# An encoder of two layers in one launch: x's two halves in one padded tile, other places for the weights' tiles, and a reordered beginning and end

## The chip, the cores and the metric

The kernel runs on one core of a Trainium2 chip. The metric is the time of one execution on the device in microseconds, as the median of several runs. The engines of the core are named as in the profile: PE (TensorE, matrix products; PEld is its loading of weights), DVE (VectorE), ACT (ScalarE), POOL (GpSimd) and SP (SyncE, which here only issues transfers). Memory on the chip is SBUF, with 128 partitions; products land in PSUM.

## What is computed

A sequence of 512 positions, 1024 features wide, goes through two layers. Each layer is a mixer and an MLP, both added to x; layer 0 mixes by stick-breaking attention, layer 1 by a gated linear recurrence. At the end there is a norm.

```python
def rms_norm(x, g):
    y = x * rsqrt(mean(x * x, axis=-1, keepdims=True) + EPS)
    return y * g

for layer in range(2):
    h = rms_norm(x, norm_mix[layer])
    if layer == 0:
        y = stick_breaking_attention(h, sb_w_qkv[0], sb_w_o[0])
    else:
        y = rglru_block(h, rg_w_in[0], conv_w, conv_b, w_a, b_a, w_x, b_x, lam, rg_w_o[0])
    x = x + y
    h = rms_norm(x, norm_mlp[layer])
    x = x + square(relu(h @ w1[layer])) @ w2[layer]        # 1024 -> 4096 -> 1024
return rms_norm(x, norm_final)
```

All is float32.

## The kernel before

**Every product in three.** A float32 operand is split into a high and a low half, each in the format fp32r: `wh` is a cast of the raw weights on ACT, `wl` the difference raw - wh on DVE. The same is done to the activations: x times its norm's gains lies in `xgh` and `xgl` (`halves`, L126), mixer outputs and MLP hidden values in `bh` and `bl` (and `sh`, `sl`). `three` (L217) then issues three matmuls: wh with the high half, wl with the high half, wh with the low half. In a matmul one operand is loaded into PE as 128 columns of weights (the stationary or loaded operand) and the other one is streamed through, 256 or 512 columns long. In `three` the weights slab is loaded and x is streamed.

**Stages.** (1) A beginning, in which x and the first slabs of weights arrive and the first products for queries and keys start. The norm's factor is found beside them: `inverse` (L432) sums squares on PE (L436), takes the root on ACT, and on DVE makes a diagonal matrix `diag` and the factors `rp` and `rn`, which PE broadcasts (L453). (2) Attention in 8 pairs of heads, where PE's work (`fill`) is cut into steps, and the steps of scores and values are put among them at due times. `SUMS` and `BROAD` say after which fill step the two parts of `inverse` are placed. (3) The MLP of layer 0. (4) The recurrent block, in an order written out by hand. (5) The MLP of layer 1, and (6) the final norm, row block by row block, as the last products come out.

**The MLP.** The class `Mlp` does Strassen's seven products in place of eight. For the first quarter of the hidden width, `squared` (L828) computes plainly 8 slabs of `w_m1`, each with 24 matmuls of 512 columns in `dense` (L223). Then follow, in turn, a down stage (`times`, L1051, 14 steps of 12 matmuls of 512 columns) and an up stage (`up`, L956, 2 halves `p` of 7 products, each of 24 matmuls of 256 columns): down, up, down, up, down, up, down. In an up stage P1, P2 and P4 stream parts of `xgh` and `xgl`, P7 streams `xgh` and `low`, P5 and P3 stream `s41` and `low`, P6 streams parts of `bh` and `bl` and `low`; the weights are loaded. In a down stage the roles are changed: hidden values are loaded (`bh` and `bl` for the first half, `sh` and `sl` for the second, from `places`, L845) and weights are streamed. `leave` (L1185) runs after each step and issues what ACT and DVE do with its bank: in an up stage P1's bank is copied out (L1209) before P6 adds to the same bank, P4's bank goes through relu and square (L1219), and then `prepare` makes operands for a step four ahead. Inside these stages ACT and DVE run strictly in the order in which the code issues work (`Ordered`, L747), and all of it is recorded at L756.

**Places in SBUF.** Pools lay their tiles one behind the other in the order in which they are opened, so a longer tile moves everything behind it. Each of `xgh`, `xgl`, `bh` and `bl` is 16384 bytes per partition. The pool `last` (L1583) lies ahead of the tiles of layer 1's MLP only.

**The end.** `square` adds up squares of a half row block on ACT, `finish` (L1631) takes the root, scales the one half on ACT (the gains multiplied in by POOL in `scaled`, L1627), the other on DVE, and issues both stores on SP. `end` (L1649) puts these among the last products; row block 3, half 0, comes last, in two parts of 256 columns.

Of the kernel before, what the change touches and what calls it, by code (L numbers as in the profile page):

```python
# [17 lines left out]
P = 128  # L18
S = 512
# [7 lines left out]
SCALE = HD ** -0.5  # L27

# [13 lines left out]
SUMS = 5  # L42
BROAD = 9
# [18 lines left out]
def hybrid_encoder(  # L62
# [57 lines left out]
    xgh = const.tile([P, C, S], F32R, tag="xgh", name="xgh")  # L120
    xgl = const.tile([P, C, S], F32R, tag="xgl", name="xgl")
# [56 lines left out]
    def slab_parts(src, cuts):  # L178

        raw = wpool.tile([P, C, P], F32, tag="raw", name="raw", bufs=3)  # L180
        wh = wpool.tile([P, C, P], F32R, tag="wh", name="wh")
        wl = wpool.tile([P, C, P], F32R, tag="wl", name="wl")

        def fetch(i, queue=nc.sync):
            k = slice(*cuts[i : i + 2])
            queue.dma_start(out=raw[:, k, :], in_=src[:, k, :])

        def part(i, high=A.copy):
            k = slice(*cuts[i : i + 2])
# [4 lines left out]
            V.tensor_tensor(wl[:, k, :], raw[:, k, :], f(wh[:, k, :]), ALU.subtract)  # L194

        return wh, wl, fetch, part
# [93 lines left out]
    with ExitStack() as actx:  # L290
# [141 lines left out]
        def inverse():  # L432
# [9 lines left out]
            with tc.high_priority():  # L442
                norm["root"] = A.activation(rc, pc[:, :NB], AF.Sqrt, bias=eps_t, scale=1.0 / D)
                V.reciprocal(rc, rc)
                for t in range(NB):
                    ts = slice(t * P, (t + 1) * P)
                    V.tensor_scalar(diag[:, ts], ident, rc[:, t : t + 1], None, ALU.mult)
                V.tensor_scalar(rp, rc, SCALE, None, ALU.mult)
                V.tensor_scalar(rn, rc, -SCALE, None, ALU.mult)
# [289 lines left out]

    residual(w_so, "mlp0", so, so_next)  # L740
# [25 lines left out]
    class Mlp:  # L766
# [28 lines left out]
        def __init__(self, ctx, layer):  # L795
# [12 lines left out]
            self.s41 = self.bp.tile([P, C // 2, S], F32R, tag="s41", name="s41", bufs=1)  # L808
# [288 lines left out]
        def run(self, first, between, end):  # L1097
# [87 lines left out]
            def leave(i):  # L1185
# [32 lines left out]
                if name == "P4":  # L1218
                    self.A.activation(u[3], three, AF.Relu)  # L1219
                    self.square(u[3])  # L1220
                    if p:
                        last_sums(u, self.SUMS[:2])
                if later:
                    later.pop()()
# [19 lines left out]
                elif name == "P4":  # L1244
                    self.sums(p, slice(0, 2))
# [66 lines left out]
    with ExitStack() as mctx:  # L1312
# [18 lines left out]
        def end(ws, xs):  # L1331
            for i in range(2):
# [244 lines left out]

    residual(w_ro, "mlp1", begun, {4: ws["o4"]})
# [3 lines left out]
    with ExitStack() as mctx:  # L1582
        lp = mctx.enter_context(tc.tile_pool(name="last", bufs=1))  # L1583
# [26 lines left out]
        A.activation(lp.tile([P, 1], F32, tag="rt", name="early"), eps_t, AF.Sqrt)  # L1610

        ss = lp.tile([P, NB, 3], F32, tag="ss", name="ss")
        bias = lp.tile([P, NB], F32, tag="bias", name="bias")

        def square(t, h, i, cols=slice(0, S), end=False):

            junk = work.tile([P, S], F32, tag="sq", name="junk")
            A.activation(
                junk[:, cols], mlp.y(t, h)[:, cols], AF.Square, accum_out=ss[:, t, i : i + 1]
            )  # L1620
            if not end:
                A.activation(
# [4 lines left out]
        def scaled(t, h, cols=slice(0, S)):  # L1627
            y = mlp.y(t, h)[:, cols]
            G.tensor_tensor(y, y, gb[h][:, cols], ALU.mult)

        def finish(t, h, i, cut=None, last=None):  # L1631

            ts = slice(t * P, (t + 1) * P)
            rt = work.tile([P, 1], F32, tag="rt", name="rt")
            A.activation(rt, ss[:, t, i : i + 1], AF.Sqrt, bias=bias[:, t : t + 1], scale=1.0 / D)
            V.reciprocal(rt, rt)
            done, y = mlp.y(t, 1 - h), mlp.y(t, h)
            A.activation(done, done, AF.Copy, scale=rt)
            nc.sync.dma_start(out=out[ts, (1 - h) * S : (2 - h) * S], in_=done)
            with tc.issue_after(last.ins) if last else nullcontext():  # L1640
                V.scalar_tensor_tensor(
# [3 lines left out]
            if cut:  # L1645
                V.tensor_scalar(y[:, :cut], y[:, :cut], rt, None, ALU.mult)
            nc.sync.dma_start(out=out[ts, h * S : (h + 1) * S], in_=y)

        def end(ws, xs):  # L1649
            for t in range(2):  # L1650
# [13 lines left out]
            for i in range(2):  # L1664
                cols = slice(i * HS, (i + 1) * HS)
                ps = mlp.bank()[:, :HS]
                for g in range(2):
                    mlp.times("P4", g, 1, ws[g], ps, True, cols)
                mlp.collect("P4", 1, ps, cols)
                square(3, 0, 1 + i, cols, end=i == 1)  # L1670
                if i == 0:
                    scaled(3, 0, cols)
            finish(3, 0, 2, HS)
# [72 lines left out]
```

## Time and profile before

| | |
|---|---|
| median of 3 runs | 1047.62 us (1046.17 to 1047.67) |
| the profiled execution | 1047.03 us, its span 1045.3 us |
| granted clock of TensorE | 0.998 of full speed |
| one up stage, layer 0 and layer 1 | 39.42 and 39.84 us |
| last operation on the chain | ACT's scaling at 1040.54 us, 0.72 us |
| HBM | 137.41 MB read, 4.19 MB written, 135 GB/s over the span |

Times in the views are counted from the span's start. A row of a group has line, engine, operation, the tiles `out<-in`, and its number; for a matmul the first tile behind the arrow is the streamed one, the second the loaded one. A row of the waits view says who waited for whom, how long in total, how often, and the longest.

### The profile page before, as it was taken

The page shows a single profiled execution, that of the slowest core. Times are in us where ns is not written, and L with a number is a line of the kernel's source. Part 1 is how long each engine was busy: PE and PEld are TensorE (multiplying, and loading weights), DVE is VectorE, ACT ScalarE, POOL GpSimd, SP SyncE. Part 2 cuts the span into 40 slices and gives each one's busy share as a digit, 9 for nine tenths or more (in the row PEclk, how much of TensorE's full clock was granted, in tenths as well). Part 3 has the DMA queues.
Part 4 walks back from the last instruction along what each step waited for, and adds up shares of the span by engine and source line. Part 5 has one row for each costly group of instructions (what it writes and reads, how often), then busy time and mean ns, then how long its engine had stood idle before and what let it go on. Part 6 is the DMA issues. An engine that isn't in the chain of part 4 may idle for free.

```text
span 1045.3 us, 15858 instructions
## 1 busy us (share of the span) xinstructions
PE 1033.3 (99%) x5868; PEld 901.0 (86%) x5868; DVE 862.5 (83%) x1150; ACT 702.4 (67%) x1082; POOL 170.3 (16%) x235
## 2 busy tenths in 40 slices
PE   9999999999999999999999999999999999999997
PEld 7888888888888988988988888888888988988985
DVE  7788787847788898898899799984789797897897
ACT  6767676835766773773775699964755773773775
POOL 0354344420000010010011111100000010010013
PEclk9999999999999999999999999999999999999999
DMA  7755454537646667667682474353346667567563
GB/s 232 196 139 142 102 152 104 152 108 284 144 78 189 180 139 209 156 142 208 163 208 78 129 204 114 89 221 101 81 89 174 178 135 208 161 135 204 149 123 101
DMA packets 52828, 159.41 MB, mean 152 GB/s; under 512 B 6672, under 2 KB 7952, under 8 KB 52752
## 3 DMA queue, kind: packets, MB, share of 16 engines
q1 hardware_dynamic: 41808, 120.13, 35.5%
q0 software_dynamic: 10368, 37.75, 21.8%
q8 instruction: 46, 0.75, 0.3%
q10 hardware_dynamic: 576, 0.52, 0.2%
q14 instruction: 30, 0.25, 0.1%
HBM read 137.41 MB, written 4.19 MB: 135 GB/s over the span
## 4 chain that ended last, share of the span: by engine, by line
PE 85%; DVE 6%; issue 3%; DMA 3%; ACT 2%; SPq 1%; ACTq 0%; DVEq 0%; POOL 0%; POOLq 0%
PE ps_t L1060 14%; PE ps_acc L965 8%; PE ps_z L965 8%; PE ps_acc L1060 7%; PE ps_o L965 5%; PE ps_acc L221 5%; PE ps_acc L219 5%; PE ps_acc L220 5%; PE ps_z L1060 4%; PE ps_t L220 2%; PE ps_t L221 2%; PE ps_t L219 2%; PE ps_o L219 2%; PE ps_o L220 2%; PE ps_o L221 2%
## 5 line engine op out<-in xcount | busy, mean ns | idle before, releaser
L756 ACT CAST wh<-b 128x1024 fp32r<-128x1024 f32 x168 | 174.1, 1048 | 125.4 <-DVE b L756 77.7
L756 DVE TENSOR_TENSOR wl<-b,wh 128x1024 fp32r<-128x1024 f32 x168 | 203.6, 1220 | 50.4 <-ACT wh L756 50.2
L1042 POOL DMA_DIRECT2D b<-in_w_dn x40 | 35.0, 875 | 360.4 <-DVE b L756 204.5
L219 PE MATMUL ps_acc<-xgh,wh 128*128 128x512 f32 x192 | 78.5, 409 | 0.0
L214 DVE TENSOR_TENSOR wl<-raw,wh 128x512 fp32r<-128x512 f32 (+2 forms) x70 | 62.0, 912 | 18.3 <-ACT wh L212 18.2
L221 PE MATMUL ps_acc<-xgl,wh 128*128 128x512 f32 x192 | 75.2, 391 | 0.0
L220 PE MATMUL ps_acc<-xgh,wl 128*128 128x512 f32 x192 | 75.1, 391 | 0.0
L580 DVE TENSOR_TENSOR_SCAN scan<-keep,later 128x128 f32<-128x128 f32 (+1 forms) x64 | 58.6, 919 | 18.2 <-ACT keep L570 11.4
L756 ACT ACTIVATE u<-u 128x512 f32<-128x512 f32 x100 | 63.1, 632 | 6.9 <-DVE u L756 5.1
L212 ACT CAST wh<-raw 128x512 fp32r<-128x512 f32 (+2 forms) x70 | 50.6, 758 | 24.5 <-PE ps_acc L221 7.3
L584 POOL TENSOR_TENSOR w<-w,scan 128x128 f32<-128x128 f32 (+1 forms) x64 | 51.8, 812 | 58.6 <-DVE scan L580 52.0
L1042 POOL DMA_DIRECT2D b<-in_w_up x24 | 20.8, 868 | 240.6 <-DVE b L756 72.2
L756 DVE TENSOR_TENSOR b<-b,b 128x1024 f32<-128x1024 f32 x48 | 58.7, 1223 | 1.3
L756 DVE TENSOR_TENSOR u<-u 128x512 f32<-128x512 f32 (+1 forms) x92 | 54.8, 596 | 2.7 <-ACT u L756 1.1
L965 PE MATMUL ps_z<-xgh,wh 128*128 128x256 f32 x192 | 54.2, 282 | 0.0
L965 PE MATMUL ps_z<-xgh,wl 128*128 128x256 f32 x192 | 54.1, 282 | 0.0
L756 ACT CAST wh<-raw 128x1024 fp32r<-128x1024 f32 x46 | 47.9, 1046 | 9.2 <-PE ps_acc L1060 8.4
L965 PE MATMUL ps_acc<-low,wh 128*128 128x256 f32 x192 | 53.6, 279 | 0.0
L1060 PE MATMUL ps_t<-wl,sh 128*128 128x512 f32 x126 | 50.1, 398 | 0.0
L1060 PE MATMUL ps_t<-wh,sh 128*128 128x512 f32 x126 | 49.6, 394 | 0.0
L1060 PE MATMUL ps_t<-wh,sl 128*128 128x512 f32 x126 | 49.4, 392 | 0.0
L1060 PE MATMUL ps_t<-wh,bh 128*128 128x512 f32 x126 | 49.2, 391 | 0.0
(397 smaller groups left out, 3420.3 us busy)
## 6 DMA issues: line engine op xcount, KB each, us to landing
b<-in_w_dn SPq DMA_DIRECT2D x48, 512.0 KB, 4.5
b<-in_w_dn POOLq DMA_DIRECT2D x40, 512.0 KB, 5.6
b<-in_w_up SPq DMA_DIRECT2D x36, 512.0 KB, 4.7
b<-in_w_up POOLq DMA_DIRECT2D x24, 512.0 KB, 5.5
raw<-in_w_m SPq DMA_DIRECT2D x16, 512.0 KB, 4.1
raw<-in_w_dn SPq DMA_DIRECT2D x16, 512.0 KB, 4.6
raw<-in_w_in SPq DMA_DIRECT2D x16, 512.0 KB, 4.2
raw<-in_w_qk SPq DMA_DIRECT2D x12, 512.0 KB, 3.8
```

The costliest lines, as they stand in the source:

```text
L212: A.copy(wh[:, k, :], raw[:, k, :])
L214: V.tensor_tensor(wl[:, k, :], raw[:, k, :], f(wh[:, k, :]), ALU.subtract)
L219: PE.matmul(ps, wh, ah, start=start, stop=False)
L220: PE.matmul(ps, wl, ah, start=False, stop=False)
L221: PE.matmul(ps, wh, al, start=False, stop=stop)
L580: V.tensor_tensor_scan(sc[:, S - n : S][:, ::-1], keep[:, :n][:, ::-1], later[:, S - n :][:, ::-1], 1.0, ALU.mult, ALU.max,)
L584: G.tensor_tensor(wt, wt, sc[:, S - n + 1 : S + 1], ALU.mult)
L756: ins = getattr(self.e, name)(*args, **kwargs)
L965: PE.matmul(ps[:, i * HS : (i + 1) * HS], m, y, start=new and i == k == n == 0, stop=i == 1 and k == C // 2 - 1 and n == 2, skip_group_che ...
L1042: G.dma_start(out=unit[b].rearrange("p j n -> p (j n)"), in_=unit["src"](to), accum_op=ALU.add)
L1060: PE.matmul(ps, m, y[:, jj, cols], start=first and n == 0, stop=last and n == 2, skip_group_check=not new,)
```

## The change

It has four parts.

1. **Places.** `xgh` and `xgl` become two views into one tile `xg` that is `ASIDE` = 16 elements (64 bytes) longer. `x_at(ASIDE)` sets the views 64 bytes from the tile's start for attention and the recurrent block, `x_at(0)` sets them at its start for the two MLPs. `s41` gets 64 bytes of padding behind it. The pool `last` is gone; its small tiles now lie in unused columns of `colt` and in `c`.
2. **Beginning.** `SUMS` and `BROAD` go up by one step, and the low halves of the value weights are no longer issued with the high ones, but after `rn` and after the broadcast's copy.
3. **Later relu.** In an up stage's first half, relu, square and the sums for P4 are put off to the next step.
4. **End.** Its operations on ACT and DVE are issued in a fixed order, the last gain of tile row 3's other half moves ahead, the product with the final gains for tile row 3 goes from POOL to DVE, and the last store is issued by ACT.

```diff
+ASIDE = 16
...
-SUMS = 5
-BROAD = 9
+SUMS = 6
+BROAD = 10
...
-    xgh = const.tile([P, C, S], F32R, tag="xgh", name="xgh")
-    xgl = const.tile([P, C, S], F32R, tag="xgl", name="xgl")
+    x_t = const.tile([P, 2 * C * S + ASIDE], F32R, tag="xg", name="xg")
+    xgh = xgl = None
+
+    def x_at(aside):
+
+        nonlocal xgh, xgl
+        xgh, xgl = (
+            x_t[:, aside + i * C * S : aside + (i + 1) * C * S].rearrange("p (c s) -> p c s", s=S)
+            for i in range(2)
+        )
+
+    x_at(ASIDE)
...
-        def part(i, high=A.copy):
+        def part(i, high=A.copy, low=True):
...
-            if high == V.tensor_copy:
+            if high == V.tensor_copy or not low:
                 return
...
-                V.tensor_scalar(rn, rc, -SCALE, None, ALU.mult)
+                norm["signs"] = V.tensor_scalar(rn, rc, -SCALE, None, ALU.mult)
...
-                for u, name in zip(parts[4:], ("root", "copy")):
+                for u, name, then in zip(parts[4:], ("root", "copy"), ("signs", "copy")):
 
                     with tc.issue_after(norm[name].ins):
                         for i in range(2):
-                            u[3](i)
+                            u[3](i, low=False)
+                    with tc.issue_after(norm[then].ins):
+                        for i in range(2):
+                            u[3](i, None)
...
+    x_at(0)
     residual(w_so, "mlp0", so, so_next)
...
-            self.s41 = self.bp.tile([P, C // 2, S], F32R, tag="s41", name="s41", bufs=1)
+            t = self.bp.tile([P, C // 2 * S + ASIDE], F32R, tag="s41", name="s41", bufs=1)
+            self.s41 = t[:, : C // 2 * S].rearrange("p (k s) -> p k s", s=S)
...
                 if name == "P4":
-                    self.A.activation(u[3], three, AF.Relu)
-                    self.square(u[3])
+                    def fourth(u=u, three=three, p=p):
+                        self.A.activation(u[3], three, AF.Relu)
+                        self.square(u[3])
+                        if p:
+                            last_sums(u, self.SUMS[:2])
+                        else:
+                            self.sums(p, slice(0, 2))
+
                     if p:
-                        last_sums(u, self.SUMS[:2])
-                if later:
+                        fourth()
+                    else:
+                        later.append(fourth)
+                elif later:
                     later.pop()()
...
-                elif name == "P4":
-                    self.sums(p, slice(0, 2))
...
         def end(ws, xs):
+            x_at(ASIDE)
...
+    x_at(0)
     residual(w_ro, "mlp1", begun, {4: ws["o4"]})
...
-        lp = mctx.enter_context(tc.tile_pool(name="last", bufs=1))
         mlp = Mlp(mctx, 1)
...
-        def scaled(t, h, cols=slice(0, S)):
+        def scaled(t, h, cols=slice(0, S), e=G):
             y = mlp.y(t, h)[:, cols]
-            G.tensor_tensor(y, y, gb[h][:, cols], ALU.mult)
+            e.tensor_tensor(y, y, gb[h][:, cols], ALU.mult)
...
         def end(ws, xs):
             for t in range(2):
                 square(t, 0, 0)
                 scaled(t, 0)
                 square(t, 1, 1, end=True)
-                finish(t, 1, 1, last=mlp.gained)
+                rt = root(t, 1)
+                scaled_half(t, 0, rt, nc.sync)
+                whole_half(t, 1, rt, last=mlp.gained)
             for t in range(2, 4):
                 square(t, 1, 0)
-                scaled(t, 1)
+            scaled(2, 1)
             for g in range(2):
                 mlp.times("P4", g, 0, ws[g], xs[0], False)
+            mlp.collect("P4", 1, xs[1])
+            for e in (EV, EA):
+                e.turn(True)
+            mlp.V = EV
             mlp.collect("P4", 0, xs[0])
             square(2, 0, 1, end=True)
-            finish(2, 0, 1)
-            mlp.collect("P4", 1, xs[1])
...
+            mlp.collect("P4", 1, ps[0], halves[0])
+            rt = root(2, 1)
+            square(3, 0, 1, halves[0])
+            scaled_half(2, 1, rt, nc.sync)
+            whole_half(2, 0, rt)
+            mlp.collect("P4", 1, ps[1], halves[1])
+            square(3, 0, 2, halves[1], end=True)
+            scaled(3, 1, e=EV)
+            scaled(3, 0, halves[0], e=EV)
+            rt = root(3, 2)
+            whole_half(3, 0, rt, HS)
+            scaled_half(3, 1, rt, A)
```

The new helpers `root`, `scaled_half` and `whole_half` are the three parts of `finish`; `scaled_half` takes the queue on which its store is issued.

What it moves is seen in the order of the instructions. On DVE in the beginning, from the reciprocal of the norm's root on (`diag`, `rp`, `rn` go to PE's broadcast and to the scores; `wl` are low halves of value weights), before and then after:

```order
L444 RECIPROCAL rc<-rc 128x4
L194 TENSOR_TENSOR wl<-raw,wh 128x512 x2
L447 TENSOR_SCALAR diag<-ident,rc 128x128 x4
L448 TENSOR_SCALAR rp<-rc 128x4
L449 TENSOR_SCALAR rn<-rc 128x4
```

```order
L455 RECIPROCAL rc<-rc 128x4
L458 TENSOR_SCALAR diag<-ident,rc 128x128 x4
L459 TENSOR_SCALAR rp<-rc 128x4
L460 TENSOR_SCALAR rn<-rc 128x4
L205 TENSOR_TENSOR wl<-raw,wh 128x512 x2
```

The two low halves have moved from ahead of `diag` to behind `rn`. On ACT in an up stage, at the change from the first half to the second (`ps_acc` is P4's bank of the first half, `ps_z` P1's of the second), before and then after:

```order
L756 CAST bh<-u 128x2x768
L756 ACTIVATE u<-ps_acc 128x2x256
L756 ACTIVATE u<-u 128x2x256
L756 CAST wh<-b_8014 128x1024
L756 COPY u<-ps_z 128x512
L756 COPY u<-ps_o 128x512
```

```order
L771 CAST bh<-u 128x2x768
L771 CAST wh<-b_8007 128x1024
L771 COPY u<-ps_z 128x512
L771 ACTIVATE u<-ps_acc 128x2x256
L771 ACTIVATE u<-u 128x2x256
L771 COPY u<-ps_o 128x512
```

Relu and square now stand behind one cast of weights and the copy of `ps_z`; the order on DVE there is unchanged. On DVE at the end, before and then after (the four tiles `c` are the output's quarters; 7346 and, after, 7342 hold the half that comes last):

```order
L1641 SCALAR_TENSOR_TENSOR c_7346<-c_7346,rt,gb 128x512
L756 SCALAR_TENSOR_TENSOR c_7346<-ps_o,rr,c_7346 128x256
L1636 RECIPROCAL rt<-rt 128x1
L1641 SCALAR_TENSOR_TENSOR c_7346<-c_7346,rt,gb 128x256
L1646 TENSOR_SCALAR c_7346<-c_7346,rt 128x256
```

```order
L771 SCALAR_TENSOR_TENSOR c_7342<-c_7342,rt,gb 128x512
L771 SCALAR_TENSOR_TENSOR c_7342<-ps_o,rr,c_7342 128x256
L771 TENSOR_TENSOR c_7343<-c_7343,gb 128x512
L771 TENSOR_TENSOR c_7342<-c_7342,gb 128x256
L771 RECIPROCAL rt<-rt 128x1
L771 SCALAR_TENSOR_TENSOR c_7342<-c_7342,rt,gb 128x256
L771 TENSOR_SCALAR c_7342<-c_7342,rt 128x256
```

Two products that POOL did before stand on DVE ahead of the last reciprocal. The matmuls are the same 5844 in both kernels, and apart from the two parts of `inverse` they stand in the same order.

More of the change, by code (lines that the diff above doesn't have):

```diff
@@ L1625, in square, with root, leaves, scaled_half @@
                 )
-        def scaled(t, h, cols=slice(0, S)):
+        def scaled(t, h, cols=slice(0, S), e=G):
             y = mlp.y(t, h)[:, cols]
-            G.tensor_tensor(y, y, gb[h][:, cols], ALU.mult)
-        def finish(t, h, i, cut=None, last=None):
-            ts = slice(t * P, (t + 1) * P)
+            e.tensor_tensor(y, y, gb[h][:, cols], ALU.mult)
+        def root(t, i):
             rt = work.tile([P, 1], F32, tag="rt", name="rt")
[L1635 to L1639, printed above, removed]
+            EA.activation(rt, ss[:, t, i : i + 1], AF.Sqrt, bias=bias[:, t : t + 1], scale=1.0 / D)
+            EV.reciprocal(rt, rt)
+            return rt
+        def leaves(t, h, queue):
+            queue.dma_start(out=out[t * P : (t + 1) * P, h * S : (h + 1) * S], in_=mlp.y(t, h))
+        def scaled_half(t, h, rt, queue):
+            y = mlp.y(t, h)
+            EA.activation(y, y, AF.Copy, scale=rt)
+            leaves(t, h, queue)
+        def whole_half(t, h, rt, cut=None, last=None):
+            y = mlp.y(t, h)
             with tc.issue_after(last.ins) if last else nullcontext():
-                V.scalar_tensor_tensor(
+                EV.scalar_tensor_tensor(
                     y[:, cut:], y[:, cut:], rt, gb[h][:, cut:],
@@ L1645, in finish @@
             if cut:
[L1646 to L1647 removed]
+                EV.tensor_scalar(y[:, :cut], y[:, :cut], rt, None, ALU.mult)
+            leaves(t, h, nc.sync)
         def end(ws, xs):
```

25 lines of the change are left out of this document (11 added, 14 removed).

## The prediction

> **What bounds the kernel now.** I read the engine shares first, then TensorE's waits, then the chain of waits, and only then the tail.
>
> ```profile
> span 1045.3 us, 15858 instructions
> PE 1033.3 (99%) x5868; PEld 901.0 (86%) x5868; DVE 862.5 (83%) x1150; ACT 702.4 (67%) x1082; POOL 170.3 (16%) x235
> PE ps_z L965 <- ACT u L756: 1.0, 1, 1.0
> PE ps_z L453 <- DVE rn L449: 0.6, 1, 0.6
> PE ps_t L602 <- DVE tl L618: 0.4, 1, 0.4
> PE ps_z L436 <- DVE ssq L421: 0.3, 1, 0.3
> ```
>
> TensorE is busy for 99% of the span, and its waits that this change touches, the four rows above, come to 2.3 us. A change that keeps all matmuls can therefore gain only in three ways: by ending one of these waits, by shortening the tail behind the last matmul, or by making the matmuls follow each other faster. The last sounds impossible, since the granted clock is 1.00 in the windows shown further down, but the chain of waits says otherwise. It merges a run of matmuls into one row (start, length, what, count). Here is the second half of one up stage, first in layer 0 and then in layer 1; each row is one product of 24 matmuls 256 columns wide:
>
> ```profile
> 430.27 2.88 PE ps_z L965 x24
> 433.15 2.74 PE ps_o L965 x24
> 435.89 2.83 PE ps_z L965 x24
> 438.71 2.72 PE ps_o L965 x24
> ...
> 900.56 2.88 PE ps_z L965 x24
> 903.44 2.83 PE ps_o L965 x24
> 906.27 2.84 PE ps_z L965 x24
> 909.10 2.82 PE ps_o L965 x24
> 911.93 2.84 PE ps_z L965 x24
> 914.76 2.86 PE ps_o L965 x24
> 917.63 2.88 PE ps_z L965 x24
> ```
>
> The products come in the order P1, P5, P6, P3, P7, P2, P4. P1, P2 and P4 stream x's halves and take 2.86 to 2.88 us. P5 and P3 stream s41: 2.72 to 2.74 us in layer 0, but 2.82 to 2.83 in layer 1. Same code, same sizes, no wait; what differs between the layers is where s41 lies. Add up the tile sizes in pool order and take each address modulo 512 bytes: x's halves lie at 32, the weight slabs wh and wl at 288, s41 at 480 in layer 0 and at 96 in layer 1 (the pool `last` sits ahead of it there). So the distance from the loaded operand to the streamed one is 256 for x, 192 for s41 in layer 0, 320 in layer 1. The matmuls of 512 columns in the down stages depend on it as well (layer 0, then layer 1; each 12 matmuls):
>
> ```profile
> 452.75 2.72 PE ps_acc L1060 x12
> 455.47 2.75 PE ps_t L1060 x12
> ...
> 923.25 2.72 PE ps_acc L1060 x12
> 925.97 2.80 PE ps_t L1060 x12
> ```
>
> In each pair the first row loads bh (distance 256 in both layers), the second loads sh: distance 320 in layer 0, 192 in layer 1. So for 512 columns 256 is the cheap distance and 192 the dear one (2.80/12 = 233 ns a matmul against 227); for 256 columns it is the other way round, 2.73/24 = 114 ns at 192 against 2.87/24 = 120 at 256.
>
> **The change part by part: places.** The tile `xg` is 64 bytes longer than the two it replaces, so everything behind it moves by 64: wh and wl to 352, bh to 96. Outside the MLPs x begins at 96 (distance 256, as before). In the MLPs it begins at 32, so the distance becomes 192. s41 comes to 32 in both layers, since `last` is gone: 192. Its own pad puts sh and sl at 96: 256 in both layers.
>
> - Up stages, x: P1, P2 and P4 go from 2.88, 2.86 and 2.88 to s41's 2.73, P7, half of which streams x, from 2.84 to 2.73. That is 0.15 + 0.13 + 0.15 + 0.11 = 0.54 us a half, in 2 halves of 6 stages: -6.4 us. P6 streams bh and stays. No row has x at 192, so the bounds are s41's two layers: at 2.73 it is this, at 2.82 only 0.06 + 0.04 + 0.06 + 0.02 = 0.18 a half, -2.2 us. I take the first, because it is the row with the same distance and the same width. A loss is excluded only by there being no 24-matmul row dearer than x's own 2.88.
> - Up stages, s41 of layer 1: from 2.83 and 2.82 to 2.73, 0.19 a half in 6 halves: -1.1 us.
> - Down stages: sh serves 7 products of 12 matmuls a quarter, 28 a layer. Layer 1 from 2.80 to 2.73: -2.0 us; layer 0 from 2.75 to 2.73: -0.6 us.
> - The price: 8 slabs of w_m1 a layer are 24 matmuls of 512 columns, each streaming x. Between these two rows lie 22 matmuls in 5.00 us, 227 ns each:
>
> ```profile
> 725.22 0.40 PE L220 MATMUL ps_acc<-xgh,wl 128*128 128x512 f32 x1
> 730.22 0.40 PE L221 MATMUL ps_acc<-xgl,wh 128*128 128x512 f32 x1
> ```
>
> At 192 I expect sh's 233: 6 ns x 24 x 16 = +2.3 us (nothing if the penalty belongs to sh alone).
>
> Sum of the places: -6.4 - 1.1 - 2.6 + 2.3 = -7.8 us.
>
> [...]
>
> Is anything else too slow to follow? In these windows, one up stage of each layer, VectorE works 31.9 us of 39.8 (the columns are the length, then each engine's busy time and count):
>
> ```profile
> 410.38:449.80 39.42, 39.42 (x337) 39.42 (x336) 31.75 (x32) 28.73 (x38) 3.49 (x4) 1.00 0.61 154
> 880.46:920.30 39.84, 39.84 (x337) 39.84 (x336) 31.92 (x32) 28.85 (x39) 3.48 (x4) 1.00 0.59 152
> ```
>
> With 1.5 us less the stage is about 38.4 us, and VectorE at 83% keeps up; a load late by a fraction of a product would show as a new wait.
>
> **Beginning.** The four sums of squares and the broadcast stand one step (3 matmuls, 0.68 us) later on TensorE. On VectorE the two `wl` slabs leave the path from the reciprocal to `rn`:
>
> ```profile
> 25.01 0.17 DVE L444 RECIPROCAL rc<-rc 128x4 f32<-128x4 f32 x1
> 25.09 1.26 DVE L194 TENSOR_TENSOR wl<-raw,wh 128x512 fp32r<-128x512 f32 x2
> 26.27 0.86 DVE L447 TENSOR_SCALAR diag<-ident,rc 128x128 f32<-128x128 f32 x4
> 27.13 0.16 DVE L449 TENSOR_SCALAR rn<-rc 128x4 f32<-128x4 f32 x1
> ```
>
> `rn` is then there 1.2 us sooner and is wanted 0.7 us later, so the waits of 0.6 and 0.3 both go: -0.9 us. Behind the moved slabs wait the first value products, some 5 us later; that cover hides them, and without it they would cost their 1.2 us. Bounds: 0, if the later wait of 0.4 on `tl` (L618) grows by what was gained, and -1.3, if it goes too.
>
> **Later relu.** The wait of 1.0 us at L965 is for the fourth of these rows:
>
> ```profile
> 824.49 0.59 ACT L756 ACTIVATE u<-ps_acc 128x512 f32<-128x512 f32 x1
> 825.11 0.63 ACT L756 ACTIVATE u<-u 128x512 f32<-128x512 f32 x1
> 825.65 1.03 ACT L756 CAST wh<-b 128x1024 fp32r<-128x1024 f32 x1
> 826.59 0.58 ACT L756 COPY u<-ps_z 128x512 f32<-128x512 f32 x1
> ```
>
> P6 adds into a bank that this copy must read first. Relu and square (1.2 us) go behind the copy, which then ends near 826.0 instead of 827.2: -1.0 us, once. At the five other places the copy is in time already, so the move gives nothing there. What is queued behind the moved pair: the copy of ps_o, read by P3 a whole product later, and VectorE's four sums, which started at 827.9 and now wait for a square that ends near 827.3. Bounds 0 and -1.2.
>
> **End.** VectorE first, then GpSimd and the output queue:
>
> ```profile
> 1033.81 0.74 DVE L1641 SCALAR_TENSOR_TENSOR c<-c,rt,gb 128x512 f32<-128x512 f32 x1
> 1034.66 1.60 DVE L1641 SCALAR_TENSOR_TENSOR c<-c,rt,gb 128x512 f32<-128x512 f32 x1
> 1036.18 0.74 DVE L756 SCALAR_TENSOR_TENSOR c<-ps_t,rr,c 128x512 f32<-128x512 f32 x1
> 1040.88 0.35 DVE L1646 TENSOR_SCALAR c<-c,rt 128x256 f32<-128x256 f32 x1
> ...
> 1032.67 3.04 POOL L1629 TENSOR_TENSOR c<-c,gb 128x512 f32<-128x512 f32 x2 [1.04 <-ACT junk L1618]
> ...
> 1039.44 2.18 SPq L1639 DMA_DIRECT2D out<-c  x2
> 1041.71 0.38 SPq L1647 DMA_DIRECT2D out<-c  x1
> ```
>
> The same operation takes 0.74 us, and 1.60 while GpSimd's second product runs. That product (tile row 3) goes to VectorE, behind the last gain. So the gain at 1036.18 starts 0.8 us sooner, about when its matmuls end, and the chain square, root, reciprocal moves with it. The two products added to VectorE (by the 0.74, some 0.7 + 0.4 us) sit where it waits 0.9 us for the last root, and cost 0.2. The two last stores no longer follow each other on one queue: the last issue stood 0.5 us behind its data (1041.71 against 1041.23). Together -0.8 + 0.2 - 0.4, about -1.0 us; bounds -0.2, if the second queue issues no sooner, and -1.2. The rest (one load ahead of another on SyncE, small tiles in `colt` and `c`) is covered by TensorE's 99%.
>
> **Sum.** -7.8 - 0.9 - 1.0 - 1.0 = -10.7 us against the profiled execution's own 1047.03 us: 1036.3. The median is 0.6 above that execution, so the forecast is 1037.0 us.
>
> **Rivals.**
>
> - Places do nothing (8%): the two streams do not meet, and what sets the layers apart is what the other engines do meanwhile. Then beginning, relu and end are left, 1047.6 - 2.9 = 1044.7 us. For it: VectorE's load does differ a little between the two windows (31.75 and 31.92 us). Against: 0.1 us a product between the s41 rows of the layers, while the rows of x are alike in both.
> - x gets only what s41 has in layer 1 (10%): -2.2 instead of -6.4, so 1037.0 + 4.2 = 1041.2 us. For it: the unseen pair of places. Against: the equal distance.
> - Slower (6%): it is not the distance but the place of the loaded tile that counts, and 96 modulo 256 is the dear one, as for sh in layer 1. Then wh, wl and bh, now all there, cost every 512-column matmul 6 ns: about 1500 dense ones and 666 on bh +13 us, sh of layer 0 +1.3, the gains of the up stages open (counted as nothing): 1047.6 + 14.3 - 2.9 = 1059 us. It decides if a dense slab takes 5.6 us instead of 5.46. [...]
>
> **How the numbers follow.** The forecast has 76%, its own range 1034.0 to 1040.5: 1037.0 less the better bounds of the three waits (0.8) and the price that may not come (2.3), and more by their worse ones (0.9, 1.0 and 0.8) and part of x's. The 8-in-10 range reaches to the x rival with some room: 1034.0 to 1042.5. 0.2% is 2.1 us, about what a measurement here tells from no change. Forecast and both mild rivals are faster by more, less a little for the first rival lying only 2.9 away: faster 0.91, same 0.03, slower 0.06.
>
> **What would show it.** Right: rows of 24 at 2.73 for P1, P2, P4, P5 and P3 in both layers; down rows of 12 at 2.72 to 2.75 everywhere; w_m1 slabs at 5.6; the waits at L965, L453 and L436 gone; the last store issued about 1 us after its data less. Wrong: x's rows still at 2.86, dense slabs slower outside the MLPs, or a new wait on VectorE in the up stages.

## The result, and the profile after

The changed kernel takes 1041.79 us (median of 6 runs, 1041.42 to 1043.37), the kernel before 1046.89 us beside it; the ratio is 0.9955 with a 95% interval of 0.9942 to 0.9968. So it is faster, by 5.1 us where 10.6 were forecast, and lies near the upper edge of the range. The profiled execution took 1041.67 us. Its page:

```profile
span 1040.0 us, 15867 instructions
PE 1030.8 (99%) x5868; PEld 900.0 (87%) x5868; DVE 861.4 (83%) x1152; ACT 701.9 (67%) x1082; POOL 173.2 (17%) x233
```

Its waits of TensorE from 790 us on (who waited for whom: in total, how often, the longest):

```profile
PE ps_z L981 <- ACT u L771: 0.8, 1, 0.8
PE ps_acc L981 <- ACT u L771: 0.3, 1, 0.3
PE ps_t L1076 <- DVE wl L771: 0.3, 1, 0.3
```

The waits for `rn`, `ssq` and `tl` of the beginning are no longer listed in its whole view. The wait for the copy of P1's bank in an up stage (now L981) is still there, and two small ones are new. The chain of waits through the same half of an up stage as before, layer 0 and then layer 1 (start, length, what, count):

```profile
427.97 2.83 PE ps_z L981 x24
430.80 2.83 PE ps_o L981 x24
433.62 2.83 PE ps_z L981 x24
436.45 2.83 PE ps_o L981 x24
...
900.73 2.83 PE ps_o L981 x24
903.55 2.83 PE ps_z L981 x24
906.38 2.83 PE ps_o L981 x24
909.21 2.83 PE ps_z L981 x24
912.03 2.83 PE ps_o L981 x24
```

This is where the forecast failed. Every product shown takes 2.83 us (the first row of layer 0 is P1, the last of layer 1 is P2): x came from 2.86 to 2.88 to 2.83, not to 2.73, and s41 of layer 0 *lost* its 2.73 although its distance did not change. The down stages did what was forecast: 2.72 us for the product with bh and for the one with sh behind it, in both layers (layer 0, then layer 1, again from the chain of waits):

```profile
450.48 2.72 PE ps_acc L1076 x12
453.20 2.72 PE ps_t L1076 x12
...
920.40 2.72 PE ps_acc L1076 x12
923.12 2.72 PE ps_t L1076 x12
```

So did the end. In the timeline of ScalarE the last store is issued 0.03 us behind the scaling that it stores (before, 0.5 us):

```profile
1035.19 0.72 ACT L771 ACTIVATE c<-c,rt 128x512 f32<-128x512 f32 x1 [0.23 <-DVE rt L771]
1035.94 0.38 ACTq L1665 DMA_DIRECT2D out<-c  x1
```

The start of one matmul to the start of the next, as a mean over the records of the up stages (layer 0 / layer 1; the few starts behind a wait, over 150 ns, are left out), says it in nanoseconds:

| streamed | before | after |
|---|---|---|
| x | 119.3 / 119.4 | 117.7 / 116.5 |
| s41 | 113.9 / 118.5 | 117.5 / 116.9 |
| all of the stage | 117.4 / 118.7 | 117.8 / 116.9 |

In layer 0 the stage got no faster at all; the price in w_m1 was paid in full (226.9 to 233.3 ns a matmul in layer 0, 227.6 to 233.3 in layer 1). Between these two rows lie the same 22 matmuls of w_m1 as those of the prediction, now in 5.14 us where it had 5.00:

```profile
722.66 0.39 PE L231 MATMUL ps_acc<-xg,wl 128*128 128x512 f32 x1
727.80 0.39 PE L232 MATMUL ps_acc<-xg,wh 128*128 128x512 f32 x1
```

### The profile page after: what moved, and what is told of

Its sections match the earlier page's. It is cut to its first block, busy times and chain, and to the rows that moved or that the text cites. A ratio compares the mean times of both kernels' runs of the same rounds, so it can differ in the third digit from the quotient of the medians.

```text
span 1040.0 us, 15867 instructions
## 1 busy us (share of the span) xinstructions
PE 1030.8 (99%) x5868; PEld 900.0 (87%) x5868; DVE 861.4 (83%) x1152; ACT 701.9 (67%) x1082; POOL 173.2 (17%) x233
## 4 chain that ended last, share of the span: by engine, by line
PE 87%; DVE 6%; ACT 3%; issue 2%; DMA 1%; POOL 0%; DVEq 0%; ACTq 0%; POOLq 0%
PE ps_t L1076 13%; PE ps_acc L981 8%; PE ps_acc L1076 7%; PE ps_z L981 7%; PE ps_acc L230 5%; PE ps_acc L231 5%; PE ps_acc L232 5%; PE ps_o L981 4%; PE ps_z L1076 3%; PE ps_t L231 2%; PE ps_t L230 2%; PE ps_t L232 2%; DVE wl L771 2%; PE ps_o L230 2%; PE ps_o L231 2%
## 5 line engine op out<-in xcount | busy, mean ns | idle before, releaser
L230 PE MATMUL ps_acc<-xg,wh 128*128 128x512 f32 x192 | 78.7, 410 | 0.0
L231 PE MATMUL ps_acc<-xg,wl 128*128 128x512 f32 x192 | 75.4, 393 | 0.0
L232 PE MATMUL ps_acc<-xg,wh 128*128 128x512 f32 x192 | 75.3, 392 | 0.0
L981 PE MATMUL ps_z<-xg,wh 128*128 128x256 f32 x336 | 67.1, 281 | 0.0
L981 PEld LDWEIGHTS ps_z<-xg,wh 128*128 128x128 f32 x336 | 54.4, 189 | 0.1
L981 PE MATMUL ps_acc<-low,wh 128*128 128x256 f32 x192 | 53.9, 281 | 0.0
L981 PE MATMUL ps_z<-xg,wl 128*128 128x256 f32 x192 | 53.8, 280 | 0.0
L981 PE MATMUL ps_acc<-xg,wh 128*128 128x256 f32 x240 | 49.2, 280 | 0.0
```

The source lines that it names most:

```text
L230: PE.matmul(ps, wh, ah, start=start, stop=False)
L231: PE.matmul(ps, wl, ah, start=False, stop=False)
L232: PE.matmul(ps, wh, al, start=False, stop=stop)
L981: PE.matmul(ps[:, i * HS : (i + 1) * HS], m, y, start=new and i == k == n == 0, stop=i == 1 and k == C // 2 - 1 and n == 2, skip_group_che ...
```

## The experiments

### First set: what is the distance worth, and to whom

**Matmuls alone.** None of the encoder's work: 96 pairs of places at two widths (6 loaded, 16 streamed), each with 12 matmuls of 256 and 12 of 512 columns, nothing else running, in one execution.

```python
for b in LOADED:                       # 32, 96, 160, 288, 352, 480
    for a in STREAMED:                 # 0, 32 ... 480
        for cols in (256, 512):
            ...                        # 12 matmuls: wh*high, wl*high, wh*low
```

> A map, no encoder: it leaves out the whole computation and issues only matmuls in the pattern of three (12 to a group), with the streamed operand at each of 16 places 32 bytes apart and the loaded operand at 32, 96, 160, 288, 352 and 480 bytes modulo 512, for 256 and for 512 columns. Theory A (the distance alone sets the spacing): equal distances give equal times, whatever the places, with 114 ns at distance 192 for 256 columns and 233 ns for 512. Theory B (the two places count, not only their distance): at the same distance of 192 the pair 480 over 288 gives about 114 ns and the pair 32 over 352 about 117.5 ns, as in the kernel before and the changed one. Theory C (what the other engines do to SBUF meanwhile sets it): with PE alone the map is flat.

Measured, as mean ns from start to start, by streamed place minus loaded place modulo 256 bytes (each figure is the middle one of 12 pairs):

```
distance      0     32     64     96    128    160    192    224
256 columns 118.6  116.9  113.3  119.8  119.8  117.2  115.1  118.6
512 columns 229.2  233.4  228.6  233.5  233.4  234.0  232.6  232.7
```

In eight of the sixteen columns the twelve pairs agree to 0.4 ns; in each of the others one or two fall out, among them the first groups of all (305 and 338 ns). So it is the distance that counts, neither place by itself, and with no other engine at work; and it repeats after 256 bytes. That ends the rival of the dear place 96. Two odd pairs of 256 columns at 192 run at 117.7, however, where the other ten run at 115.1 (four matmuls of 116 to 122, then 113.3). They are the streamed place 32 over the loaded places 96 and 352, and the second is x's own pair in the changed kernel, as theory B had it. The next two runs rule that theory out: there s41 at 32 over 352 is fast, and x at 480 over 288 is not. What the two odd pairs have of their own was the thread to pull.

**x's place taken back.** The changed kernel with x at the same distance in the MLPs as elsewhere; everything else of the change stays.

```diff
-    x_at(0)
     residual(w_so, "mlp0", so, so_next)
...
-            x_at(ASIDE)
...
-    x_at(0)
     residual(w_ro, "mlp1", begun, {4: ws["o4"]})
```

> The changed kernel with x left 64 bytes from its tile's start in the MLPs too (distance 256 there): beginning, end, later relu and the other places stay. If x's move is worth what the changed kernel's rows say (117.5 instead of 119.5 ns for 1056 matmuls of 256 columns, 233 instead of 227 for 384 of 512 columns), it is the same within 0.1% of the changed kernel: -2.1 us against +2.3 us, so about 1042.0 us. If the forecast's -6.4 + 2.3 were still hidden behind another wait, it would be 4 us slower, 1046.

Measured: 1039.54 us, ratio to before 0.9927 (0.9914 to 0.9939). That is 2.3 us faster than the changed kernel by the medians, and the intervals of the two ratios lie apart: the part of the change from which most of the gain was forecast costs time. Its chain, layer 1:

```profile
896.49 2.88 PE ps_z L980 x24
899.36 2.74 PE ps_o L980 x24
902.10 2.83 PE ps_z L980 x24
904.93 2.72 PE ps_o L980 x24
907.65 2.83 PE ps_z L980 x24
910.48 2.86 PE ps_o L980 x24
913.34 2.88 PE ps_z L980 x24
```

x is back at 2.88 and s41 (the rows of 2.74 and 2.72) is back at its fast pace, now in layer 1 too. x slow and s41 fast, or both at 2.83: the sum is nearly the same, and only the second pays for w_m1.

**x alone moved**, in the kernel before: to 480, which is distance 192 of the loaded 288.

```diff
-    xgh = const.tile([P, C, S], F32R, tag="xgh", name="xgh")
-    xgl = const.tile([P, C, S], F32R, tag="xgl", name="xgl")
+    x_t = const.tile([P, 2 * C * S + 128], F32R, tag="xg", name="xg")
...
+    x_at(128)
...
+    x_at(112)
     residual(w_so, "mlp0", so, so_next)
```

> The kernel before, with x alone moved in the MLPs to 480 bytes modulo 512 (32 elsewhere, as before), the weights at 288: s41's own pair of places in layer 0. Theory B: x's products of 24 come down from 2.87 to 2.73 us as s41's, -6.4 us, and w_m1's slabs rise to 233 ns a matmul, +2.3 us: 4.1 us faster than before. Theory A with a floor of its own for x (117.5 at distance 192): -2.1 + 2.3, the same as before. Theory C: no change in the rows.

Measured: 1048.09 us, ratio 1.0012 (1.0003 to 1.0021), slower by some 1.6 us (in its trace a wait for the copy of P1's bank has also grown, from 1.0 to 2.0 us). The same change of rhythm in layer 0, s41 included, whose place was not touched at all:

```profile
430.26 2.83 PE ps_z L976 x24
433.09 2.83 PE ps_o L976 x24
435.92 2.83 PE ps_z L976 x24
438.74 2.83 PE ps_o L976 x24
```

So what x does sets the pace of s41 behind it: x came down to 2.83 and no further, and s41 went up from 2.73 to 2.83.

**The beginning alone**, in the kernel before.

```diff
-SUMS = 5
-BROAD = 9
+SUMS = 6
+BROAD = 10
...
-                            u[3](i)
+                            u[3](i, low=False)
+                    with tc.issue_after(norm[then].ins):
+                        for i in range(2):
+                            u[3](i, None)
```

> The kernel before with the changed beginning alone. The forecast's term: the waits of 0.6 and 0.3 us are gone, -0.9 us. The changed kernel's trace suggests more: 2.7 us ahead by 60 us from the start, so if it is the beginning and not the places that gains there, -2.7 us; if the places give part of it, between the two.

Measured: 1045.15 us, ratio 0.9984 (0.9975 to 0.9993). All three waits of the beginning go from the waits view, the 0.4 us for `tl` (L602) too.

### Second set: two rhythms

**Runs of 72 matmuls behind four kinds of start**, again without any of the encoder's work, in one execution.

```python
for ahead in ("wide", "x", "P6", "stall"):
    for n in range(3):
        for far, low in ((192, 192), (64, 64), (64, 192)):
            ...                        # what goes ahead, n matmuls longer each time
            run(72, far, low, 256)
```

> Matmuls alone: runs of 72 matmuls of 256 columns at three pairs of distances (both streamed halves at 192, both at 64, the high half at 64 and the low at 192), each behind 12 matmuls of 512 columns at distance 0, behind 24 of 256 columns at 0, behind 24 with the high half at 0 and the low at 192 (P6's pattern), and behind a wait of TensorE. Theory D, two rhythms: at distance 192 a run goes at 113.5 ns a matmul or at 117.6, the one it falls into when it begins, and keeps it for all 72; at 64 there is only 113.3; 64 with 192 lies at 117 to 119, as s41 of layer 1 before. Rival E, distance alone with the other engines' traffic on top: every run at 192 goes at one and the same spacing (115 in the map's mean), whatever came ahead of it. Rival F: the spacing belongs to the first dozen matmuls only, and all runs at 192 end at 113.5.

In equal stretches of 7 us inside the runs, PE's count tells the pace (window, its length, then PE's busy time and count). Distance 192: the first two rows behind wide matmuls (512 columns), one behind 24 at distance 0, two behind P6's pattern, two behind a wait; then two runs at 64:

```profile
57.50:64.50 7.00, 7.00 (x62) 7.00 (x61) 0.00 (x0) 0.00 (x0) 0.00 (x0) 1.00 0.00 0
92.10:99.10 7.00, 7.00 (x62) 7.00 (x61) 0.00 (x0) 0.00 (x0) 0.00 (x0) 1.00 0.00 0
127.00:134.00 7.00, 7.00 (x64) 7.00 (x63) 0.00 (x0) 0.00 (x0) 0.00 (x0) 1.00 0.01 2
229.00:236.00 7.00, 7.00 (x64) 7.00 (x64) 0.00 (x0) 0.00 (x0) 0.00 (x0) 1.00 0.00 0
297.00:304.00 7.00, 7.00 (x62) 7.00 (x61) 0.00 (x0) 0.00 (x0) 0.00 (x0) 1.00 0.01 2
332.50:339.50 7.00, 7.00 (x62) 7.00 (x61) 0.00 (x0) 0.00 (x0) 0.00 (x0) 1.00 0.00 0
369.50:376.50 7.00, 7.00 (x64) 7.00 (x63) 0.00 (x0) 0.00 (x0) 0.00 (x0) 1.00 0.00 0
...
138.00:145.00 7.00, 7.00 (x62) 7.00 (x62) 0.00 (x0) 0.00 (x0) 0.00 (x0) 1.00 0.00 0
240.20:247.20 7.00, 7.00 (x62) 7.00 (x61) 0.00 (x0) 0.00 (x0) 0.00 (x0) 1.00 0.00 0
```

64 matmuls or 62, and nothing between: by their starts 113.3 ns or 117.8, kept to the end of the run. At 192 the run is fast behind x's distance 0 in 3 of 3, behind P6's pattern in 2 of 3, behind a wait in 2 of 3, and slow behind wide matmuls at distance 0 in the two tries in which these followed each other at 227 ns (the third, the first run of all, came out of wide matmuls at 427 ns and was fast). At 64 all twelve runs, and with the low half at 192 all twelve, go at 117.8; the map's 113.3 at 64 is the other rhythm, met there behind wide matmuls at distance 32. The runs at distance 0 ended at 120 ns. Theory D holds for 192 and falls for 64.

**x, s41 and low at 64**, by the map's figure, in the changed kernel.

```diff
-    x_t = const.tile([P, 2 * C * S + ASIDE], F32R, tag="xg", name="xg")
+    x_t = const.tile([P, 2 * C * S + 48], F32R, tag="xg", name="xg")
...
-            self.acc = work.tile([P, S], F32, tag="ssq", name="ssq", bufs=1)
+            self.acc = work.tile([P, S + 32], F32, tag="ssq", name="ssq", bufs=1)[:, :S]
...
-            t = self.bp.tile([P, C // 2 * S + ASIDE], F32R, tag="s41", name="s41", bufs=1)
+            t = self.bp.tile([P, C // 2 * S + 48], F32R, tag="s41", name="s41", bufs=1)
```

> The changed kernel with x, s41 and low 64 bytes beyond the loaded weights' place (modulo 256) in the MLPs instead of 64 ahead of it; bh, bl, sh, sl stay at distance 0. Theory D: the 256-column rows that stream x, s41 or low go at 113.3 ns (2.72 us for 24) in both layers, 5 ns less than x has beside the padded tile: 1039.5 - 88 x 6.1 ns x 12 halves (6.4 us), + 0.9 for w_m1's 384 matmuls at 229 instead of 227, + 0.6 for the recurrent block's slabs that come to 192: about 1034.5 us. Rival E (distance matters less here than in the map, since the other engines read and write too): 117.5 ns as in the changed kernel, 1041. If the faster stages wait for VectorE, about 1 us more than the first.

Measured: 1043.25 us, ratio 0.9960 (0.9946 to 0.9974): a miss of 9 us for the map's figure of 256 columns. All products of layer 0 stand at 2.83 to 2.85, the slow rhythm again (here P1, which streams x, and P5, which streams s41); w_m1 alone came as the map has it for 64, at 229.0 ns:

```profile
426.84 2.83 PE ps_z L981 x24
429.66 2.83 PE ps_o L981 x24
```

**The same with relu in its old place.**

```diff
                     else:
-                        later.append(fourth)
-                elif later:
+                        self.A.activation(u[3], three, AF.Relu)
+                        self.square(u[3])
+                if later:
...
+                elif name == "P4":
+                    self.sums(p, slice(0, 2))
```

> The same with relu and square of P4 back in their old place. Theory G, the later relu still saves the wait for P1's copy once a layer 1 stage: 0.3 to 1 us slower than the run with it. Rival H, the later relu brings the waits for VectorE near 844 and 856 us: without it those waits are gone and it is up to 1 us faster.

Measured: 1044.73 us against 1043.25, 1.5 us slower. TensorE's waits from 790 us on, first of this kernel, then of x_at_64:

```profile
PE ps_z L981 <- ACT u L771: 1.5, 1, 1.5
PE ps_acc L981 <- ACT u L771: 0.3, 1, 0.3
PE ps_t L1076 <- DVE wl L771: 0.2, 1, 0.2
```

```profile
PE ps_acc L981 <- ACT u L771: 0.3, 1, 0.3
PE ps_t L1076 <- DVE wl L771: 0.2, 1, 0.2
```

The later relu takes away the large wait; the two small ones stand in both.

**The later relu alone**, in the kernel before.

```diff
-                    self.A.activation(u[3], three, AF.Relu)
-                    self.square(u[3])
-                    if p:
-                        last_sums(u, self.SUMS[:2])
-                if later:
+                    def fourth(u=u, three=three, p=p):
+                        ...
+                    if p:
+                        fourth()
+                    else:
+                        later.append(fourth)
+                elif later:
```

> The kernel before with nothing but the later relu. Theory as forecast: the wait of 1.2 us at the first up stage of layer 1 goes, -1.0 us, 1045.5. Rival, from the changed kernel's trace: the wait stays at 0.9 us since the copy is late for another reason (the stage's chain starts with a load that lands late), -0.3 us, 1046.2, which 11 runs hardly tell from nothing.

Measured: 1045.50 us, ratio 0.9989 (0.9980 to 0.9998): 1.0 us, as forecast, though its own trace still shows 0.4 of the wait, and one of 0.2 for `wl` in a down stage that the kernel before does not show.

### Third set: half of x in the fast rhythm

**x in two parts.** P1 and P7 stream chunks 0 to 3 and stay at distance 0, to put what follows into the fast rhythm; P2 and P4 stream chunks 4 to 7, now at 192.

```diff
-    x_at(0)
+    x_at(48)
...
+            self.parts = [
+                x_t[:, o : o + C // 2 * S].rearrange("p (c s) -> p c s", s=S)
+                for o in (at, at + C // 2 * S + far)
+            ]
```

> x in two parts: in the MLPs chunks 0 to 3 (P1, P7) stay at distance 0 of the loaded weights, chunks 4 to 7 (P2, P4) lie at 192; everything else as beside the padded tile (1039.5). Theory D (at 192 the rhythm of 113.4 or 117.8 ns is the one a run falls into, and behind a product at 0, or the mix of 0 and 192 that P6 and P7 stream, it is mostly the fast one): P5 behind P1 and P3 behind P6 stay at 113.4, P2 behind P7 and P4 behind P2 come from 119.6 to 113.4, rows of 24 at 2.72 to 2.73 us: 48 x 6.2 ns x 12 halves = -3.6, and half of w_m1's 384 matmuls 6 ns dearer, +1.1: about 1037.1 us. Rival I (x cannot go faster than 117.8, only s41 can): -1.0 + 1.1, 1039.6.

**The control:** the same with chunks 4 to 7 at 64.

```diff
-    x_at(48)
+    x_at(16)
```

> The control: the same with chunks 4 to 7 at distance 64, where a run behind P6's mix or behind 0 always went at 117.8 ns in the matmuls alone. Theory D: P2 and P4 at 117.8, rows of 2.83 us, -1.0 us, w_m1 +0.4: about 1038.9 us, and s41 as fast as in x_split. Rival (the map's figure for 64, 113.3 ns, holds here): as fast as x_split without half its price, 1036.5.

One stretch of 5.3 us inside P2 and P4, first of the split at 192, then of the control (columns as above):

```profile
421.90:427.20 5.30, 5.30 (x49) 5.30 (x49) 4.55 (x5) 3.51 (x5) 0.86 (x1) 1.00 0.62 141
```

```profile
422.80:428.10 5.30, 5.30 (x47) 5.30 (x46) 4.17 (x5) 3.82 (x6) 0.84 (x1) 1.00 0.62 102
```

As expected of the two rhythms: x at 192 now runs at 113.3 ns in layer 0 and 114.2 in layer 1, at 64 at 117.8 in both, and s41 stays fast in both kernels (in the control's layer 0 2.74 us for P5 and 2.72 for P3). The same distance that made x no faster than 117.7 in layer 0 of the changed kernel gives 113.3 behind a product that brings the fast rhythm. The times: 1039.96 us, ratio 0.9941 (0.9929 to 0.9953), and for the control 1040.77, ratio 0.9946 (0.9934 to 0.9958). The rows came as expected and the time did not: 1037.1 was expected of the first. The up stages are 3.4 us shorter than in x_beside, where all other distances are the same (some 1000 matmuls a layer, by 1.8 and by 1.6 ns), w_m1 takes back 1.3 (384 by 3.5 ns, where 1.1 was expected), and 1.7 went into four more waits of TensorE, here by the waits, the windows and VectorE's timeline of x_split:

```profile
PE ps_t L1087 <- DVE wl L782: 0.6, 3, 0.3
```

```profile
369.30:386.50 17.20, 17.04 (x76) 13.82 (x75) 15.76 (x20) 11.34 (x17) 2.62 (x3) 1.00 0.80 150
```

```profile
382.51 1.22 DVE L782 TENSOR_TENSOR b<-b,b 128x1024 f32<-128x1024 f32 x1
383.64 0.69 DVE L782 TENSOR_TENSOR sl<-u,sh 128x512 fp32r<-128x512 f32 x1
384.90 2.36 DVE L782 TENSOR_TENSOR wl<-b,wh 128x1024 fp32r<-128x1024 f32 x2 [0.57 <-ACT wh L782]
```

In the first 17 us of a down stage VectorE is busy for 15.76 of 17.20 us, and near their end TensorE waits for a `wl`: 0.3 us and 0.1 of slow first matmuls, in five down stages by the starts of the matmuls, one of which x_beside has too. VectorE is as full there in x_beside (15.81 us in the same stretch) and in the kernel before (15.76), and the control has that wait in one stage only. So the busy share alone does not make the wait. What differs is that TensorE gets there sooner, with up stages of 38.84 us in place of 39.46.

**One sum ahead of two gains**, to end these waits.

```diff
                     if p:
+                        if ahead < len(steps) and steps[ahead][0] == "down":
+                            add(ahead, 0)
                         for n in range(2):
                             self.collect(name, n, bank[n])
```

> x_split with one VectorE operation moved in each down stage: the sum of two weight tiles (b<-b,b, 1.2 us) that the third last wl but one needs stands ahead of the two gains (c<-ps_t,rr,c, 1.4 us) instead of behind them. Theory J (the faster up stages reach the next down stage before VectorE has its wl, five waits of 0.3 us with 0.1 us of start-up behind each, 2.1 us in all, and that is why x_split stands level with the kernel beside it): ScalarE's cast then starts 1.3 us sooner, VectorE's idle 0.6 us ahead of that wl goes, and so do the waits: 1040.0 - 2.1 = 1037.9 us. Rival (VectorE has no time to spare there, 92% of that stretch, so the wait goes to a later wl; or the banks, read 1.2 us later, make TensorE wait): 1039.5 to 1040.5 us.

Measured: 1040.20 us, ratio 0.9930 (0.9918 to 0.9942), level with x_split. The rival holds: TensorE now waits one product earlier, for the gains that were put back (by the starts of the matmuls again in five stages, of which the view lists two).

```profile
PE ps_t L1087 <- DVE c L782: 0.3, 2, 0.2
```

**The end alone**, in the kernel before, with the pool `last` left where it was.

```diff
+        EV, EA = Ordered(V), Ordered(A)
...
+            for e in (EV, EA):
+                e.turn(True)
...
+            scaled(3, 1, e=EV)
+            scaled(3, 0, halves[0], e=EV)
+            rt = root(3, 2)
+            whole_half(3, 0, rt, HS)
+            scaled_half(3, 1, rt, A)
```

> The kernel before with the end alone. As forecast: the tail behind the last matmuls 1.0 us shorter (in the changed kernel's trace 0.85), 1045.6 us. Rival: the second queue issues no sooner and the tail keeps all but 0.2 us.

Measured: 1045.14 us beside 1046.00, ratio 0.9993 (0.9984 to 1.0001): 0.9 us, as forecast, though alone it can hardly be told from nothing.

None is the fastest for certain: x_beside, x_split and x_split_sum_first (0.9927, 0.9941, 0.9930) have intervals that overlap. x_beside beats both kernels of this case and is the simplest.

## Where the prediction was right, and the step that failed

**Right in direction and in five of its seven terms.** By the runs of one part alone: beginning -1.4 us (forecast -0.9; the wait for `tl` did not grow but went too, which the bounds allowed), later relu -1.0 (-1.0), end -0.9 (-1.0). By the matmuls' starts: down stages from 230.9 to 227.0 ns in layer 1 and from 228.1 to 226.8 in layer 0, over some 655 matmuls each -2.6 and -0.9 us (-2.0 and -0.6), and w_m1 +2.3 (+2.3). x_beside, which has all of it but x's move and its price, came out 7.0 us faster than before; the forecast's terms for it (s41 of layer 1, down stages, beginning, relu, end) add up to 6.6.

**Wrong in the terms of x and s41 in the up stages: -7.5 us forecast, -1.5 measured.** The step that failed is "I take the first, because it is the row with the same distance and the same width": s41's 2.73 in layer 0 was read as a property of distance 192. It is one of two rhythms at that distance, 113.3 and 117.8 ns in two_rhythms, and s41 had it because x ran ahead of it at distance 0. x's 2.88 was the price of s41's 2.73. With x moved to 192, the up stage starts from the wide matmuls of the down stage, falls into the slow rhythm of 117.8 ns and stays there: x gains 0.13 us a half instead of 0.54 (P1, P2 and P4 0.05, 0.03 and 0.05, P7, which streams x in two of three matmuls and not in half, nothing), which is -1.6 us in all; P5 and P3 of layer 0 lose 0.2 a half, +1.2; and s41 of layer 1, which was to gain 1.1, stays at 2.83. That is -0.4 where these terms said -7.5. In the first up stage of layer 1 both halves fell into the fast rhythm behind a wait (of 0.3 and 0.8 us; x's matmuls went at 114.0 ns), which brought another 1.1 us and is why that layer stands at 116.9 (PE's count in 10 us, first such a stretch, then an ordinary one):

```profile
809.90:819.90 10.00, 10.00 (x91) 10.00 (x90) 7.83 (x8) 6.69 (x9) 0.86 (x1) 1.00 0.72 204
886.50:896.50 10.00, 10.00 (x87) 10.00 (x87) 8.53 (x9) 6.55 (x9) 0.88 (x1) 1.00 0.66 185
```

The trace of before held a hint that the rows of whole products hide: by the tile sizes `low` in P5 and P3 lay at distance 192 in both layers, and its matmuls there took 113.5 ns in layer 0 and 116.4 in layer 1.

**The sum.** With -1.5 for the up stages, -3.5 for the down stages, +2.3 for w_m1 and the three runs of one part alone, the parts add up to -6.0; -5.1 was measured. The changed kernel kept a wait of 0.8 us for the copy of P1's bank, which by the forecast was to end, and the down stage behind it took 0.5 us more than before (39.41 against 38.90). The difference may lie there; each of the three runs is also uncertain by about 0.9 us.

**The rivals.** The first rival, that places do nothing, falls by the map: 113 to 120 ns for the same matmul by distance alone, with no other engine at work. The rival "x gets only what s41 has in layer 1" gave 1041.2 us, nearest to the 1041.8 measured, but not by its mechanism: x did get 2.83, while s41 paid for it, and it counted on s41's gain in layer 1, which did not come. That 1041.79 lies inside the range is luck in the same way: the range reached there for this rival, not for what happened. The dear place 96 is excluded by the map and by the down stages at 2.72.

**The cover.** "VectorE at 83% keeps up" held for the changed kernel, whose up stages did not get shorter in layer 0. It would not have held for the forecast: x_split, with half of the forecast's gain in its rows, already waits for VectorE in five down stages. The 83% is a mean over the up stage; the waits came at the start of the next down stage, where VectorE stands at 92% in the kernel before too and has little to spare when TensorE comes 0.6 us sooner. That the forecast's faster stages would have met these waits is argued from x_split, not run.

**Open.** What decides which rhythm a run falls into was not found: at 192 behind P6's pattern or a wait it was fast four times in six, and at 64 the fast one was met only behind wide matmuls at distance 32. The product just ahead is not all of it: P3 follows P6, with its mix of 0 and 192, in both kernels, and went at 2.72 in layer 0 before and at 2.83 there in the changed kernel. Why the distance counts, and whether the two streams meet, which the first rival denied, no run shows. Nor was the cause of the wait of 0.8 us at L981 in the changed kernel taken apart; x_beside shows 0.4 us at another bank, and end_only, which leaves the MLPs alone, 0.8 us where the kernel before had 1.0.

## What to carry to other kernels

When two groups of matmuls of one shape run at different paces, do not give the faster pace to a property of its own (place, distance) until a run shows it without the neighbours it had: here the slow group made the fast one fast. Try such a change on one operand alone before it is bundled; x alone moved would have shown a loss in one run. And when a stage is to get shorter, look for the helper engine's cover in the stretch behind it too, where that engine is fullest, and not only in the stage's mean.

## What the runs showed of the hardware

- In map_places the spacing of back-to-back fp32r matmuls went with the distance between the streamed and the loaded tile in SBUF modulo 256 bytes: 113.3 to 119.8 ns for 256 columns and 228.6 to 234.0 for 512 as means of a dozen, at a granted clock of 0.999 and with no other engine at work.
- At distance 192 with 256 columns two_rhythms showed two steady rhythms, 113.3 and 117.8 ns, and each run of 72 matmuls kept the one it settled in at its start. Which one it was went with what was ahead, by a rule that was not found: fast in 3 of 3 behind matmuls at distance 0, in 2 of 3 behind P6's pattern and behind a wait, in 1 of 3 behind wide matmuls. At distance 64 both were met too, 113.3 in map_places and 117.8 in all twelve runs of two_rhythms.
- For 512 columns distance 0 settled at 226.6 ns after five matmuls (these five took 228 to 236); in the changed kernel, w_m1 at 192 stood at 233.3.
